# Weighted sum of two expert outputs: first loads of 16, 12, 16 and 4 tokens, merged stores of the late tiles, and a split after 108 tokens

## The chip, the cores and the metric

The kernel runs on one core of one Trainium2 chip. The metric is device time in microseconds of one execution, the median of the runs. The work is done by VectorE (DVE), ScalarE (ACT) and the core's 16 DMA engines; SyncE (SP) and ACT issue the transfers, each on a queue of its own. TensorE is not used.

## The reference

```python
expert_outputs = np.random.randn(16, 1024, 2, 512).astype(np.float32)
combine_weights = np.random.randn(16, 1024, 2).astype(np.float32)

def reference(expert_outputs, combine_weights):
    weights = combine_weights[..., np.newaxis]
    return np.sum(expert_outputs * weights, axis=2).astype(np.float32)
```

For each of 16,384 tokens two rows of 512 numbers are scaled by two weights and added. The kernel reads 67.1 MB of rows and writes 33.6 MB of sums; the weights are 131 KB.

## The kernel before

Each of the 128 partitions takes 128 tokens. A token is 4 KB of input (its two rows side by side) and 2 KB of output. `rows` (the function that cuts a tensor in DRAM) makes two regions: in the first, partition p has the tokens 120p to 120p + 119, so that the rows of two neighbouring partitions start 480 KB apart in the input and 240 KB apart in the output; in the second, the last 1,024 tokens of the tensor are dealt out eight to a partition.

The tokens of a partition go through SBUF in 11 tiles: ten of 12 tokens (`J`) and a last one of 8 (`LAST`). A tile lies in a room `et` of 48 KB in each partition. There are four rooms (`bufs=4`), used in turn, so tile g lies in the room of tile g - 4, and its load has to wait until the store of tile g - 4 has read that room.

The loads are issued on SP, line 75. The first tile has two, one of 2 tokens, cut into 4 KB pieces (`max_dma_last_dim`), and one of 10; every other tile has one, in which each partition's part is a single row of 48 KB (of 32 KB in the last tile).

At the start ACT issues a small store of zeros into places of the output that are written again later (line 58), then the weights in two transfers: those of 120 tokens, 960 B in each partition, and those of the last 8, 64 B (line 62). The first multiply on VectorE waits for the first tile's loads and for the first of these.

A tile g below 9 is combined by two instructions on VectorE. Line 84 multiplies the whole room in place with the weights, each of which is repeated 512 times by the access pattern; line 85 adds the two halves of each token and writes the sums, packed, into the front half of the same room (`ot`). Then ACT issues the store of 12 tokens, a row of 24 KB in each partition (line 86).

In tile 9 ACT scales the first half of each of 12 tokens (line 92), VectorE multiplies the second halves (line 107) and adds (line 108). In tile 10 ACT scales the first half of each of 8 tokens (line 92 again), and VectorE does the rest, one instruction per token (line 96). The stores of these two tiles are issued on SP (line 109), the last two transfers of the program.

The order on each engine is that of the program for the most part; a scheduler may move an instruction (it puts ACT's store of tile 8 among tile 9's scalings).

Of the kernel before, what the change touches and what calls it, by code (L numbers as in the profile page):

```python
# [1 line left out]

# [4 lines left out]


@with_exitstack
def kernel(  # L10
    ctx: ExitStack,
    tc: tile.TileContext,
    expert_outputs: bass.AP,
    combine_weights: bass.AP,
    out: bass.AP,
):

    nc = tc.nc  # L20
    b, s, k, h = expert_outputs.shape
    assert k == 2
    n = b * s
    P = nc.NUM_PARTITIONS
    per = n // P
    assert per * P == n
    J, LAST = 12, 8
    main = per - LAST
    assert main % J == 0
    eo = expert_outputs.rearrange("b s k h -> (b s) (k h)")  # L30
    cw = combine_weights.rearrange("b s k -> (b s) k")
    o = out.rearrange("b s h -> (b s) h")

    def rows(x):

        a = x[0 : P * main, :].rearrange("(p t) f -> p t f", p=P)
        b = x[P * main : n, :].rearrange("(p t) f -> p t f", p=P)
        return lambda t, c: a[:, t : t + c, :] if t < main else b[:, t - main : t - main + c, :]

    eo, cw, o = rows(eo), rows(cw), rows(o)  # L40

    dt = mybir.dt.float32
    mult = mybir.AluOpType.mult
    add = mybir.AluOpType.add
    copy = mybir.ActivationFunctionType.Copy

    last = main // J

    wpool = ctx.enter_context(tc.tile_pool(name="w", bufs=1))
    ipool = ctx.enter_context(tc.tile_pool(name="in", bufs=4))  # L50

    wt = wpool.tile([P, per * k], dt)


    zt = wpool.tile([16, 128], dt)
    nc.vector.memset(zt, 0.0)  # L56
    first = out.rearrange("b s h -> (b s) h")[0 : P * main, :].rearrange("(q t) h -> q (t h)", q=16)
    ahead = nc.scalar.dma_start(out=first[:, 0:128], in_=zt)  # L58

    with tc.issue_after(ahead.ins):  # L60
        for t, c in ((0, main), (main, LAST)):
            nc.scalar.dma_start(
                out=wt[:, k * t : k * (t + c)].rearrange("p (t k) -> p t k", k=k), in_=cw(t, c)
            )
        warm = wpool.tile([P, 1], dt)
        nc.scalar.activation(out=warm, in_=nc.const_aps.tensor(1.0, (P, 1), dt), func=copy)  # L66

    for g in range(last + 1):
        et = ipool.tile([P, J, k * h], dt)

        ot = et.rearrange("p j f -> p (j f)")[:, 0 : J * h].rearrange("p (j f) -> p j f", f=h)
        t0, c = g * J, J if g < last else LAST

        for a, m in ((0, 2), (2, c - 2)) if g == 0 else ((0, c),):
            nc.sync.dma_start(  # L75
                out=et[:, a : a + m],
                in_=eo(t0 + a, m),
                max_dma_last_dim=k * h * 4 if g + a == 0 else None,
            )
        if g < last - 1:  # L80

            wb = wt[:, g * J * k : (g + 1) * J * k].unsqueeze(2).to_broadcast([P, J * k, h])
            ek = et.rearrange("p j (k h) -> p (j k) h", k=k)
            nc.vector.tensor_tensor(out=ek, in0=ek, in1=wb, op=mult)  # L84
            nc.vector.tensor_tensor(out=ot, in0=et[:, :, 0:h], in1=et[:, :, h : 2 * h], op=add)  # L85
            nc.scalar.dma_start(out=o(t0, c), in_=ot)
            continue


        for i in range(c):  # L90
            t = t0 + i
            nc.scalar.activation(  # L92
                out=et[:, i, 0:h], in_=et[:, i, 0:h], func=copy, scale=wt[:, 2 * t : 2 * t + 1]
            )
            if g == last:
                nc.vector.scalar_tensor_tensor(  # L96
                    out=ot[:, i, :],
                    in0=et[:, i, h : 2 * h],
                    scalar=wt[:, 2 * t + 1 : 2 * t + 2],
                    in1=et[:, i, 0:h],  # L100
                    op0=mult,
                    op1=add,
                )
        if g < last:
            w1 = wt.rearrange("p (t k) -> p t k", k=k)[:, t0 : t0 + c, 1:2]
            x1 = et[:, :, h : 2 * h]
            nc.vector.tensor_tensor(out=x1, in0=x1, in1=w1.to_broadcast([P, c, h]), op=mult)  # L107
            nc.vector.tensor_tensor(out=ot, in0=et[:, :, 0:h], in1=x1, op=add)  # L108
        nc.sync.dma_start(out=o(t0, c), in_=ot[:, 0:c])


# [1 line left out]
_INS = ['expert_outputs', 'combine_weights']  # L113
_OUTS = [((16, 1024, 512), 'float32')]


# [23 lines left out]
```

## Time and profile before

| what | value |
|---|---|
| median of 3 runs | 239.1 us (239.07 to 240.33) |
| span of the profiled execution | 237.3 us |
| VectorE busy | 194.1 us, 29 instructions |
| ScalarE busy | 14.0 us, 22 instructions |
| DMA | 100.80 MB, mean 425 GB/s |
| first load issued by SP | 0.72 us |
| first multiply on VectorE | 18.46 us |
| first store of sums issued by ACT | 38.04 us |
| last load landed | 219.82 us |
| last store issued by SP | 226.46 us |

The costliest groups of instructions and some transfers, as the profile has them (line, engine, operation, tiles and shapes, count, then busy time and the mean of one in ns, then the idle time before them and what ended it; for transfers the size of each and the median time from issue to landing):

```profile
L84 DVE TENSOR_TENSOR et<-et,wt 128x12288 f32<-128x12288 f32 x9 | 116.6, 12955 | 24.1 <-DMA wt<-in_combine_weights_dram 17.5
L85 DVE TENSOR_TENSOR et<-et 128x6144 f32<-128x6144 f32 x9 | 59.0, 6557 | 0.3
L92 ACT ACTIVATE et<-et,wt 128x512 f32<-128x512 f32 x20 | 12.5, 708 | 208.6 <-DMA et<-in_expert_outputs_dram 208.6
L96 DVE SCALAR_TENSOR_TENSOR et<-et,wt 128x512 f32<-128x512 f32 x8 | 5.6, 746 | 3.9 <-ACT et L92 3.6
...
et<-in_expert_outputs_dram SPq DMA_DIRECT2D x9, 6144.0 KB, 29.9
out_dram<-et ACTq DMA_DIRECT2D x9, 3072.0 KB, 33.0
```

The span is what the profiler saw of one execution; the time of a run has some more around it, so the median stands above the span. Beside instructions the trace has a record of every DMA packet: one row of one partition on one of the 16 engines, with its start, its duration and its size. Where the prediction speaks of the time of a row, it is from these records.

### The profile page before, as it was taken

The page shows a single profiled execution, that of the slowest core. Times are in us where ns is not written, and L with a number is a line of the kernel's source. Part 1 is how long each engine was busy: PE and PEld are TensorE (multiplying, and loading weights), DVE is VectorE, ACT ScalarE, POOL GpSimd, SP SyncE. Part 2 cuts the span into 40 slices and gives each one's busy share as a digit, 9 for nine tenths or more (in the row PEclk, how much of TensorE's full clock was granted, in tenths as well). Part 3 has the DMA queues.
Part 4 walks back from the last instruction along what each step waited for, and adds up shares of the span by engine and source line. Part 5 has one row for each costly group of instructions (what it writes and reads, how often), then busy time and mean ns, then how long its engine had stood idle before and what let it go on. Part 6 is the DMA issues. An engine that isn't in the chain of part 4 may idle for free.

```text
span 237.3 us, 157 instructions
## 1 busy us (share of the span) xinstructions
DVE 194.1 (82%) x29; ACT 14.0 (6%) x22; POOL 0.2 (0%) x4
## 2 busy tenths in 40 slices
DVE  0008999999999999999999889969996998785710
ACT  2000000000000000000000000000000000740800
POOL 0000000000000000000000000000000000000000
DMA  7999999989899999999898999999998979999997
GB/s 289 452 474 398 398 448 480 398 356 505 352 443 435 427 464 464 398 398 530 348 514 348 447 418 443 464 464 398 398 522 348 522 344 451 464 398 442 406 434 309
DMA packets 3760, 100.80 MB, mean 425 GB/s; under 512 B 544, under 2 KB 688, under 8 KB 944
## 3 DMA queue, kind: packets, MB, share of 16 engines
q1 hardware_dynamic: 2144, 72.35, 71.0%
q10 hardware_dynamic: 1616, 28.45, 27.9%
HBM read 67.24 MB, written 33.56 MB: 425 GB/s over the span
## 4 chain that ended last, share of the span: by engine, by line
DMA 59%; DVE 34%; ACT 2%; ACTq 0%; DVEq 0%; issue 0%; SPq 0%
DMA out_dram<-et 29%; DMA et<-in_expert_outputs_dram 23%; DVE et L84 22%; DVE et L85 11%; DMA wt<-in_combine_weights_dram 7%; ACT et L92 2%; DVE et L96 1%; DVEq L135 0%; ACTq L135 0%; ACTq L58 0%; DVE zt L56 0%; DVEq L84 0%; SPq L75 0%; ACTq L92 0%
## 5 line engine op out<-in xcount | busy, mean ns | idle before, releaser
L84 DVE TENSOR_TENSOR et<-et,wt 128x12288 f32<-128x12288 f32 x9 | 116.6, 12955 | 24.1 <-DMA wt<-in_combine_weights_dram 17.5
L85 DVE TENSOR_TENSOR et<-et 128x6144 f32<-128x6144 f32 x9 | 59.0, 6557 | 0.3
L92 ACT ACTIVATE et<-et,wt 128x512 f32<-128x512 f32 x20 | 12.5, 708 | 208.6 <-DMA et<-in_expert_outputs_dram 208.6
L96 DVE SCALAR_TENSOR_TENSOR et<-et,wt 128x512 f32<-128x512 f32 x8 | 5.6, 746 | 3.9 <-ACT et L92 3.6
L107 DVE TENSOR_TENSOR et<-et,wt 128x6144 f32<-128x6144 f32 x1 | 6.6, 6557 | 2.3 <-DMA et<-in_expert_outputs_dram 2.3
L108 DVE TENSOR_TENSOR et<-et 128x6144 f32<-128x6144 f32 x1 | 6.6, 6558 | 0.9 <-ACT et L92 0.9
L66 ACT ACT_TABLE_LOAD x1 | 1.3, 1283 | 2.4 <-issue 2.4
L56 DVE MEMSET zt<- 16x128 f32 x1 | 0.2, 165 | 0.8 <-PEq L124 0.8
L66 ACT ACTIVATE warm<-const-float32-1.0 128x1 f32<-128x1 f32 x1 | 0.2, 202 | 0.0
L124 POOL MEMSET const-bfloat16-1.0<- 128x1 bf16 x1 | 0.1, 102 | 0.0
L124 POOL MEMSET const-uint8-127<- 128x1 uint8 x1 | 0.1, 101 | 0.0
L124 POOL MEMSET const-float32-0.0<- 128x1 f32 x1 | 0.1, 99 | 0.2 <-issue 0.2
L124 POOL MEMSET const-float32-1.0<- 128x1 f32 x1 | 0.1, 98 | 0.0
## 6 DMA issues: line engine op xcount, KB each, us to landing
et<-in_expert_outputs_dram SPq DMA_DIRECT2D x9, 6144.0 KB, 29.9
out_dram<-et ACTq DMA_DIRECT2D x9, 3072.0 KB, 33.0
et<-in_expert_outputs_dram SPq DMA_DIRECT2D x1, 5120.0 KB, 17.0
et<-in_expert_outputs_dram SPq DMA_DIRECT2D x1, 4096.0 KB, 25.1
out_dram<-et SPq DMA_DIRECT2D x1, 3072.0 KB, 14.6
out_dram<-et SPq DMA_DIRECT2D x1, 2048.0 KB, 10.0
et<-in_expert_outputs_dram SPq DMA_DIRECT2D x1, 1024.0 KB, 5.0
wt<-in_combine_weights_dram ACTq DMA_DIRECT2D x1, 120.0 KB, 17.0
```

What stands on the lines that cost most here:

```text
L56: nc.vector.memset(zt, 0.0)
L66: nc.scalar.activation(out=warm, in_=nc.const_aps.tensor(1.0, (P, 1), dt), func=copy)
L84: nc.vector.tensor_tensor(out=ek, in0=ek, in1=wb, op=mult)
L85: nc.vector.tensor_tensor(out=ot, in0=et[:, :, 0:h], in1=et[:, :, h : 2 * h], op=add)
L92: nc.scalar.activation(out=et[:, i, 0:h], in_=et[:, i, 0:h], func=copy, scale=wt[:, 2 * t : 2 * t + 1])
L96: nc.vector.scalar_tensor_tensor(out=ot[:, i, :], in0=et[:, i, h : 2 * h], scalar=wt[:, 2 * t + 1 : 2 * t + 2], in1=et[:, i, 0:h], op0=mul ...
L107: nc.vector.tensor_tensor(out=x1, in0=x1, in1=w1.to_broadcast([P, c, h]), op=mult)
L108: nc.vector.tensor_tensor(out=ot, in0=et[:, :, 0:h], in1=x1, op=add)
L124: nc = _bacc.Bacc("TRN2", target_bir_lowering=False, num_devices=1)
```

## The change

- The split of the tokens moves: 108 tokens of a partition lie in the first region and 20 in the second (`LAST = 20`). Rows in the first region now start 432 KB apart in the input and 216 KB apart in the output.
- The four rooms are one tile `et` of 48 tokens. They are filled first by loads of 16, 12, 16 and 4 tokens (`FIRST`), which don't end where tiles end. The first load is no longer cut into 4 KB pieces.
- The weights of the first 108 tokens are loaded on SP, right after the first load; those of the last 20 on ACT.
- The sums of tiles 7 and 8 are written side by side into one room and stored by one transfer of 24 tokens; those of tiles 9 and 10 likewise, by one of 20. Both are issued on SP. Tiles 0 to 6 are stored on ACT as before.
- Tile 9 is combined token by token (ACT scales, VectorE multiplies and adds), and tile 10 by ACT's scalings, one multiply and one add; before it was the other way round.
- The order is that of the program on every engine (`manual_schedule`).

```diff
-    J, LAST = 12, 8
+    ROOM, ROOMS = 12, 4
+    TILES = [12, 12, 12, 12, 12, 12, 12, 12, 12, 12, 8]
+    FIRST = [16, 12, 16, 4]
+    STORES = [[0], [1], [2], [3], [4], [5], [6], [7, 8], [9, 10]]
+    WHOLE = [0, 1, 2, 3, 4, 5, 6, 7, 8]
+    MIXED = [10]
+    LAST = 20
...
+    et = pool.tile([P, ROOMS * ROOM, k * h], dt)
+    halves = et.rearrange("p j (k h) -> p (j k) h", k=k)
...
+    def load(t, c, **kw):
+        at = place(t)
+        assert place(t + c - 1) == at + c - 1
+        nc.sync.dma_start(out=et[:, at : at + c], in_=eo(t, c), **kw)
...
+    def combine(g, base):
+        at, c, t0 = g % ROOMS * ROOM, TILES[g], starts[g]
+        if g in WHOLE or g in MIXED:
+            room = halves[:, k * at : k * (at + c), :]
+            x0, x1 = et[:, at : at + c, 0:h], et[:, at : at + c, h : 2 * h]
+            if g in WHOLE:
+                wb = wt[:, k * t0 : k * (t0 + c)].unsqueeze(2).to_broadcast([P, k * c, h])
+                nc.vector.tensor_tensor(out=room, in0=room, in1=wb, op=mult)
+            else:
+                for i in range(c):
+                    x = et[:, at + i, 0:h]
+                    nc.scalar.activation(out=x, in_=x, func=copy, scale=wt[:, k * (t0 + i) : k * (t0 + i) + 1])
+                w1 = wk[:, t0 : t0 + c, 1:2].to_broadcast([P, c, h])
+                nc.vector.tensor_tensor(out=x1, in0=x1, in1=w1, op=mult)
+            nc.vector.tensor_tensor(out=halves[:, base : base + c, :], in0=x0, in1=x1, op=add)
+            return
+        for i in range(c):
+            t = k * (t0 + i)
+            x0, x1 = halves[:, k * (at + i), :], halves[:, k * (at + i) + 1, :]
+            nc.scalar.activation(out=x0, in_=x0, func=copy, scale=wt[:, t : t + 1])
+            nc.vector.scalar_tensor_tensor(
+                out=halves[:, base + i, :], in0=x1, scalar=wt[:, t + 1 : t + 2], in1=x0, op0=mult, op1=add
+            )
...
+        for i, c in enumerate(FIRST):
+            load(t, c, **({} if i == 0 else {}))
+            t += c
+            if i == 0:
+                weights(nc.sync, 0, main)
...
+        for j, st in enumerate(STORES):
+            base, c = st[0] % ROOMS * ROOM * k, 0
+            for g in st:
+                combine(g, base + c)
+                c += TILES[g]
+            assert c <= k * ROOM
+            q = nc.sync if j in (7, 8) else nc.scalar
+            q.dma_start(out=o(starts[st[0]], c), in_=halves[:, base : base + c, :])
+            for g in st:
+                if g + ROOMS < len(TILES):
+                    load(starts[g + ROOMS], TILES[g + ROOMS])
```

More of the change, by code (lines that the diff above doesn't have):

```diff
@@ L26 @@
     assert per * P == n
-    J, LAST = 12, 8
+    ROOM, ROOMS = 12, 4
[5 more added lines that the diff above has]
+    LAST = 20
+    assert sum(TILES) == per and [g for st in STORES for g in st] == list(range(len(TILES)))
     main = per - LAST
[L29 to L32, printed above, removed]
+    starts = [sum(TILES[:g]) for g in range(len(TILES))]
     def rows(x):
[L36 to L40, printed above, removed]
+        first = x[0 : P * main, :].rearrange("(p t) f -> p t f", p=P)
+        second = x[P * main : n, :].rearrange("(p t) f -> p t f", p=P)
+        return lambda t, c: first[:, t : t + c, :] if t < main else second[:, t - main : t - main + c, :]
+    flat = out.rearrange("b s h -> (b s) h")
+    eo = rows(expert_outputs.rearrange("b s k h -> (b s) (k h)"))
+    cw = rows(combine_weights.rearrange("b s k -> (b s) k"))
+    o = rows(flat)
     dt = mybir.dt.float32
@@ L45 @@
     copy = mybir.ActivationFunctionType.Copy
[L47 to L63, printed above, removed]
-            )
-        warm = wpool.tile([P, 1], dt)
-        nc.scalar.activation(out=warm, in_=nc.const_aps.tensor(1.0, (P, 1), dt), func=copy)
@@ L68 @@
[L68 to L109, printed above, removed]
@@ new lines, with place @@
+    pool = ctx.enter_context(tc.tile_pool(name="all", bufs=1))
+    et = pool.tile([P, ROOMS * ROOM, k * h], dt)
+    halves = et.rearrange("p j (k h) -> p (j k) h", k=k)
+    wt = pool.tile([P, per * k], dt)
+    wk = wt.rearrange("p (t k) -> p t k", k=k)
+    zt = pool.tile([16, 128], dt)
+    warm = pool.tile([P, 1], dt)
+    def place(t):
+        g = max(g for g in range(len(TILES)) if starts[g] <= t)
+        return g % ROOMS * ROOM + t - starts[g]
+    def load(t, c, **kw):
+        at = place(t)
+        assert place(t + c - 1) == at + c - 1
+        nc.sync.dma_start(out=et[:, at : at + c], in_=eo(t, c), **kw)
@@ new lines, in weights @@
+    def weights(q, t, c):
+        q.dma_start(out=wk[:, t : t + c, :], in_=cw(t, c))
+    def combine(g, base):
[20 more added lines that the diff above has]
+                out=halves[:, base + i, :], in0=x1, scalar=wt[:, t + 1 : t + 2], in1=x0, op0=mult, op1=add
+            )
@@ new lines @@
+    with tc.manual_schedule():
+        nc.vector.memset(zt, 0.0)
+        ahead = flat[0 : P * main, :].rearrange("(q t) h -> q (t h)", q=16)
+        nc.scalar.dma_start(out=ahead[:, 0:128], in_=zt)
+        weights(nc.scalar, main, per - main)
+        nc.scalar.activation(out=warm, in_=nc.const_aps.tensor(1.0, (P, 1), dt), func=copy)
+        t = 0
+        for i, c in enumerate(FIRST):
[3 more added lines that the diff above has]
+                weights(nc.sync, 0, main)
+        assert t == sum(TILES[:ROOMS])
+        for j, st in enumerate(STORES):
[9 more added lines that the diff above has]
+                    load(starts[g + ROOMS], TILES[g + ROOMS])
```

## The prediction

> **What bounds the kernel now.** I read the page's slices and DMA queues first, then windows, then who waited for whom, and last the chain.
>
> ```profile
> span 237.3 us, 157 instructions
> ...
> DMA  7999999989899999999898999999998979999997
> ...
> q1 hardware_dynamic: 2144, 72.35, 71.0%
> q10 hardware_dynamic: 1616, 28.45, 27.9%
> HBM read 67.24 MB, written 33.56 MB: 425 GB/s over the span
> ```
>
> The two queues' packets fill 71.0 + 27.9 = 98.9% of 16 DMA engines' span, 234.7 of 237.3 us. The kernel is a full pipe: 2.6 us of the span are without packets.
>
> ```profile
> 0.00:6.00 6.00, 0.17 (x1) 1.49 (x2) 0.20 (x4) 1.00 0.78 285
> ...
> 40.00:48.00 8.00, 8.00 (x1) 0.00 (x0) 0.00 (x0) 1.00 0.98 393
> 48.00:60.00 12.00, 11.96 (x3) 0.00 (x0) 0.00 (x0) 1.00 0.99 426
> 60.00:120.00 60.00, 59.87 (x7) 0.00 (x0) 0.00 (x0) 1.00 1.00 433
> 120.00:200.00 80.00, 73.28 (x8) 0.00 (x0) 0.00 (x0) 1.00 1.01 437
> ...
> 220.00:237.30 17.30, 5.57 (x8) 4.91 (x8) 0.00 (x0) 1.00 0.91 391
> ```
>
> The columns are the stretch, its length, DVE, ACT and POOL busy time, clock, DMA share and GB/s. From 60 to 200 us the share is 1.00 or more, and nothing can be gained there but the bytes themselves. What is not full is the first 6 us (first packet at 1.79 us), a dip at 40 to 48 us, and the last 1.2 us (last packet ends at 236.1).
>
> ```profile
> DVE et L84 <- DMA wt<-in_combine_weights_dram: 17.5, 1, 17.5
> DVE et L84 <- DMA et<-in_expert_outputs_dram: 6.6, 3, 2.2
> DVE et L107 <- DMA et<-in_expert_outputs_dram: 2.3, 1, 2.3
> ```
>
> After its start at 18.46 us VectorE waits for loads 6.6 + 2.3 = 8.9 us in all. That is its slack.
>
> ```profile
> 76.96 30.61 DMA out_dram<-et
> ...
> 107.63 29.93 DMA et<-in_expert_outputs_dram
> ...
> 157.24 37.42 DMA out_dram<-et
> ...
> 194.71 25.11 DMA et<-in_expert_outputs_dram
> ```
>
> The chain runs store, load, store, load: a room is stored, then refilled. A 3 MB store takes 30 us only because its packets share the pipe with loads. The length of these pieces is the pipe's, so I cost the change in packets, not in waits.
>
> **Packets.** Every transfer has 128 rows, 8 on each engine. The trace's packet records give the median time of a row: 4 KB 159 ns (mean 194), 16 KB 611, 24 KB 912, 32 KB 1,213, 40 KB 1,514, 48 KB 1,815; a row of weights of 64 B 11 and of 960 B 44. Loads and stores of one size agree. These lie on a line: 9 ns and 36.74 ns per 1,000 B. So a 64 KB row (65,536 B) is estimated at 2,417 ns.
>
> **The change part by part, per DMA engine.**
>
> Removed: sixteen 4 KB rows (the first two tokens) 16 x 194 = 3.11 us; eight 40 KB rows 12.11; sixteen of 72 loads of 48 KB 29.04; twenty-four of 80 store rows of 24 KB 21.89; eight store rows of 16 KB 4.89; weights 8 x (44 + 11) = 0.44. Sum 71.48 us.
>
> Added: sixteen 64 KB rows 38.67; eight load rows of 16 KB 4.89; eight store rows of 48 KB 14.52; eight of 40 KB 12.11; weights of 864 and 160 B, by the line 8 x (41 + 15) = 0.45. Sum 70.64 us. Net -0.84 us.
>
> Of that, 16 x (194 - 159) = 0.56 us are slow first packets: some took about 1,000 ns at 1.8 us, when the pipe starts. Long first rows may pay part of this too. So the ends are -0.28 (all comes back) and -0.84 (none); I take -0.5, as a start is paid once by a long row, but twice or more by short ones.
>
> The price of a 64 KB row is not in the trace. Low end: the line. If it goes as two of 32 KB, 2 x 1,213 = 2,426, which adds 0.15 us over sixteen. High end: the slowest rows of the trace, 30 of 48 KB, mostly around 41 and 47 us, near 2,100 ns, 0.3 above the median; 16 x 0.3 = 4.8 us. I take the line, which six sizes fit, and keep 4.8 for the rival.
>
> **VectorE's start.** The weights of tiles 0 to 8 move from ACT's queue to SP's, behind the 16-token load. Now they land when that load does: 1.79 + 8 x 2.417 + 0.33 for the weights and about 0.9 from packet to semaphore, 22.4 us, and some 0.2 for the slow start: 22.6, against 18.46. On SP the later loads stand behind both, but nothing on SP waits there: three are issued at once, and the fourth, of four tokens, waits for the first to land, with 28 tokens still queued. VectorE is 4.1 us later, paid from its 8.9 us of slack. The first store goes at 22.6 + 19.5 = 42.1 instead of 38.04; the pipe is covered until then by first loads of 25.2 MB, which take up to 59 us. If this cover were gone, 4.1 us. Splitting tiles over loads (tile 1 needs loads one and two, tile 2 loads two and three) delays tile 2's wait a little; VectorE reaches tile 2 at 61.5 us and by then that load, 23.1 MB with half a store between, is in at about 60. Cost: nothing, under the same cover.
>
> VectorE's own work is 9 x (12.955 + 6.557) + 12 x 0.746 + 2 x 4.37 = 193.3 us against 194.1. ACT has 20 scalings as before. Stores of tiles 0 to 6 stay on ACT's queue. The refills of rooms wait for the same seven stores. Merged stores free no room that a load needs, since only loads 4 to 10 follow, after stores 0 to 6.
>
> **The end.** From tile 7 on ACT's queue is empty, so SP's alone must fill the pipe. Load 10 goes out when store 6 has landed (194.66 before). After that point load 9 had three rows of 48 KB left on each engine, 5.4 us, and load 10 is ready 1.07 us after its issue: no gap, with 4 us to spare, which store 7 filled before. Behind load 10 SP issues the store of tiles 7 and 8 (8 x 1.815 = 14.5 us), then that of 9 and 10 (8 x 1.514 = 12.1). SP waits for tile 8's sum with nothing behind it but that last store, which is later anyhow. With the last packet at 236.1 - 0.5 = 235.6, load 10's packets end near 209.0 and it lands at 209.9 (219.82 before). From there ACT's eight scalings take 5.0 us (eight in 5.01 in the timeline), alongside the multiply of 6.557 x 8/12 = 4.37; then the add, 4.37. The last store is issued at 209.9 + 9.5 = 219.4 and ready 1.07 later (0.72 to 1.79 at the start), 220.5. The 24-token store keeps the pipe busy until 209.0 + 14.5 = 223.5. So this stage costs nothing, with 3.0 us to spare. Tile 9's twelve sums on VectorE start at about 200 (tile 8 loaded at about 180.5, then 19.5) and end at 209: in time, but with little over, and they eat from the same 3 us. Without that cover the idle time would be 10.6 us.
>
> **Pitch.** Rows in HBM now lie 432 KB apart instead of 480 KB, and those of the output 216 instead of 240 KB. Packets at 480 KB show no contention from 60 to 200 us, share 1.00. Bounds: 0, and 1.9% of the loads' 156 us of packets, 3.0 us; 1.9% is what separates the span's 425 GB/s from the 433 of 60 to 120 us, the nearest thing to a slower pipe that this trace has. I take 0.
>
> The Trainium skill (DMA: Bandwidth & Descriptors, Latency and other measured facts) speaks of HBM row pitch: at large powers of two, 512 KiB among them, copies lose rate, 207 against 214 GB/s, and an odd few KiB restores it. No run here shows a pitch of 512 KiB. [...]
>
> Sum: 237.3 - 0.5 = 236.8 us of span. The median lies 1.8 above the span (239.1 - 237.3), and this stays: 238.6 us.
>
> **Rivals.**
> 1. The start and the dip both go: -0.84, and the slow rows near 41 to 47 us, which sum to 0.6 us per engine over the median, don't come again: -1.4, 237.7 us. For it: they stand once, where the first store begins, and that moment moves by 4 us. Against: a first store there will still be.
> 2. Reads are slower in the new shape (64 KB rows, 432 KB pitch). Place: every load, the first 60 us most. Price 3.0 us on all loads, or 4.8 on the long rows: 241.6 to 243.4 us. From 1.7 us on (1.1% of the loads, or 0.11 us for each long row) it decides. For it: neither shape has been seen in this trace, and the dip shows that rows can be slow. Against: six sizes on one line.
> 3. The last store comes late. Place: 219 to 224 us. If tile 9's and 10's sums are 3 us later than worked out the pipe empties, and each further microsecond is one on the end; at 6 us late 238.6 + 3 = 241.6. Against: VectorE still has 4.8 us of slack ahead.
> 4. The change does nothing in the pipe: merged stores move the same bytes. It is the forecast's own upper end, 238.8.
>
> **How the numbers follow.** About 0.5% (1.2 us) is what a measurement of this kernel tells from no change: 237.9 to 240.3 counts as the same. Forecast, with rival 4 in it, 0.46, its own range 238.0 to 239.4; rival 1, 0.24; rival 2, 0.20; rival 3, 0.10. The time is the forecast's, 238.6. The range goes from 237.3 (rival 1 less 0.4 between chips) to 241.8 (rivals 2 and 3 at their lower prices), which leaves some 0.15 out. Faster 0.24, same 0.46, slower 0.30.
>
> **What would show it.** Right: shares of the two queues summing to 98.9% or more; the first multiply at 22 to 23 us; waits of VectorE for loads down from 8.9 to about 4 to 5 us; the last load landed near 210, the last store issued near 219, and full slices to the end. Wrong: a slice under 9 tenths near 223 us (rival 3), GB/s under 420 in 2 to 60 us with full shares (rival 2), or a first 6 us with a share near 0.9 and no dip at 40 to 48 (rival 1).

## The result, and the profile after

The changed kernel takes 239.85 us (median of 18 runs, 239.59 to 240.93) against 239.13 before (18 runs): 1.0031 times as long, 95% interval 1.0023 to 1.0039. That is 0.72 us slower, where 0.5 us faster was forecast, and inside the 0.5% that was called no change. The span of the profiled execution grew from 237.3 to 237.8 us; the other 0.2 to 0.3 us lie outside it. Of all 129 runs of the kernel before, ten took 240.1 to 240.8 us and the others 239.0 to 239.5, so medians are compared.

The page after: span, busy share of the DMA engines in 40 slices, the two queues, and the bytes.

```profile
span 237.8 us, 156 instructions
...
DMA  9897999999899999999999999999898999999995
...
q1 hardware_dynamic: 2016, 78.75, 77.2%
q10 hardware_dynamic: 1184, 22.05, 21.6%
HBM read 67.24 MB, written 33.56 MB: 424 GB/s over the span
```

The shares still sum to 98.8%, though 560 packets fewer are moved (512 rows and 48 packets of 4 B): 0.988 x 237.8 = 234.95 us of packets against 234.77. Fewer rows did not make the pipe shorter. The last slice fell from 7 to 5 tenths, but that is not the loss: a packet counts in the slice in which it starts, the last rows are now 40 KB instead of 16 KB long, and the first experiment below has the same 5 at a span of 237.3 us.

The windows after (stretch, length, DVE, ACT and POOL busy, clock, DMA share, GB/s):

```profile
0.00:6.00 6.00, 0.17 (x1) 1.49 (x2) 0.20 (x4) 1.00 0.92 350
...
40.00:48.00 8.00, 8.00 (x2) 0.00 (x0) 0.00 (x0) 1.00 1.08 417
48.00:60.00 12.00, 11.96 (x2) 0.00 (x0) 0.00 (x0) 1.00 0.88 378
60.00:120.00 60.00, 59.77 (x7) 0.00 (x0) 0.00 (x0) 1.00 1.00 432
120.00:200.00 80.00, 76.73 (x9) 0.00 (x0) 0.00 (x0) 1.00 1.00 433
200.00:220.00 20.00, 19.04 (x15) 12.47 (x20) 0.00 (x0) 1.00 1.00 431
```

Here too a packet counts where it starts, and one 64 KB row on each of 16 engines is 1 MB, so the rate of a short stretch hangs on where it is cut: from 40 to 60 us these lines give 394 GB/s against 413 before, but from 36 to 56 us the same view gives 422 against 393. With each packet spread over its own duration both cuts agree: 413 GB/s from 40 to 60 us against 421 before, which is 0.4 us of the pipe. From 60 to 220 us it is 433 in both. The place to look is the first mixing of stores with loads.

Waits after, and the end of the timeline (start, length, engine, line, operation):

```profile
DVE et L83 <- DMA wt<-in_combine_weights_dram: 22.3, 1, 22.3
DVE et L83 <- DMA et<-in_expert_outputs_dram: 3.1, 2, 2.2
```

```profile
202.09 18.16 SPq L122 DMA_DIRECT2D out_dram<-et  x2
210.41 5.01 ACT L87 ACTIVATE et<-et,wt 128x512 f32<-128x512 f32 x8 [2.25 <-DMA et<-in_expert_outputs_dram]
210.42 4.43 DVE L89 TENSOR_TENSOR et<-et,wt 128x4096 f32<-128x4096 f32 x1
215.45 4.43 DVE L90 TENSOR_TENSOR et<-et 128x4096 f32<-128x4096 f32 x1 [0.60 <-ACT et L87]
```

The second wait fell from 6.6 + 2.3 to 3.1 us: VectorE paid its late start from its slack. The last load has landed at 210.3, and the last store, the second of the two on line 122, is issued at 219.90, while the 24-token store is still on the engines (until 224.4 us). There is no gap at the end.

The packet records give the ledger, in us per DMA engine. "By the line" is every row at 9 ns plus 36.74 ns per 1,000 B; "first rows" and "stall" are what rows before 8 us and after it took above that (rows over by more than 25 ns, nearly all beside the first store of sums).

```
                 by the line   first rows   stall    span
before             233.59         0.56       0.57    237.3
after              233.27         0.66       0.99    237.8
```

The saving by the line, 0.32 us, is there. The first rows cost 0.10 more, and the stall 0.42 more. The first packet starts 0.05 earlier, and the program ends 0.10 later after the last packet. The rest, 0.2 us, is not split further here: the last packets of the engines end 0.54 us apart instead of 0.43, and packets overlap by less. From 10 to 230 us 16 or more packets are under way all the time, before and after.

What else changed is that the engines no longer keep step. The semaphore records show that one transfer is reported done by the first and the last of the 16 engines 0.46 us apart before (every transfer from 75 to 196 us within 0.02 of that), and after, 1.5 to 2.2 us apart; this distance is called the spread below. The packet records show the same: before, the stores go in rounds, and between one round and the next no store row is under way for 1.37 us or more, from 44 to 200 us. In the changed kernel these pauses are 1.06 to 1.57 us until 60 us; from then on most are 0.36 us, as the rounds are stretched.

### The profile page after: what moved, and what is told of

The parts are those of the page before. It is cut to its first block, busy times and chain, and to the rows that moved or that the text cites. A ratio compares the mean times of both kernels' runs of the same rounds, so it can differ in the third digit from the quotient of the medians.

```text
span 237.8 us, 156 instructions
## 1 busy us (share of the span) xinstructions
DVE 192.3 (81%) x33; ACT 14.0 (6%) x22; POOL 0.2 (0%) x4
## 4 chain that ended last, share of the span: by engine, by line
DVE 53%; DMA 30%; issue 6%; ACT 2%; ACTq 0%; SPq 0%; another core or an unknown queue 0%; DVEq 0%
DVE et L83 38%; DVE et L90 15%; DMA out_dram<-et 15%; DMA wt<-in_combine_weights_dram 9%; DMA et<-in_expert_outputs_dram 6%; ACT et L87 2%; ACTq L151 0%; SPq L71 0%; DVEq L83 0%; ACTq L87 0%
## 5 line engine op out<-in xcount | busy, mean ns | idle before, releaser
L90 DVE TENSOR_TENSOR et<-et 128x6144 f32<-128x6144 f32 (+1 forms) x10 | 63.4, 6345 | 0.9 <-ACT et L87 0.6
L96 DVE SCALAR_TENSOR_TENSOR et<-et,wt 128x512 f32<-128x512 f32 x12 | 8.2, 745 | 0.2
L89 DVE TENSOR_TENSOR et<-et,wt 128x4096 f32<-128x4096 f32 x1 | 4.4, 4426 | 0.0
```

Of the source, the lines that this page charges most:

```text
L89: nc.vector.tensor_tensor(out=x1, in0=x1, in1=w1, op=mult)
L90: nc.vector.tensor_tensor(out=halves[:, base : base + c, :], in0=x0, in1=x1, op=add)
L96: nc.vector.scalar_tensor_tensor(out=halves[:, base + i, :], in0=x1, scalar=wt[:, t + 1 : t + 2], in1=x0, op0=mult, op1=add)
```

## The experiments

All edits are to the changed kernel unless said otherwise. Where several parts of the change were undone in a diff, only the changed lines are shown. The kernel before ran beside each, at 239.12 to 239.15 us.

**Four kernels that each undo or change one part**

```diff
-    FIRST = [16, 12, 16, 4]
+    FIRST = [12, 12, 12, 12]
```

> Only the first fill is undone: four loads of 12 tokens (48 KB rows) instead of 16, 12, 16 and 4; the weights still follow the first load on SP. In the profile of the changed kernel the packets around the first store of sums (42 to 51 us) take 0.99 us per engine more than their usual time, against 0.56 us before; the loads there are 64 KB rows. Theory A (the stall at the first store grows with the length of the load rows beside it): stall back to about 0.55 us, time 239.85 - 0.43 = 239.4 us. Theory B (the pitch of 432 and 216 KB makes it longer): stall stays near 1.0 us, time 239.8. Theory C (the merged stores at the end cost it): time 239.8. By theory A and B alike the first multiply starts near 18.3 us instead of 23.3.

Measured 239.42 us (1.0019 of before, 1.0002 to 1.0037), stall 0.49. The number is theory A's, and so the fill holds 0.43 us of the loss by the medians. Seven of the 12 runs lie below every run of the changed kernel; the other five took 240.2 to 240.7, so this run alone would not settle it, but the same fill has a low stall again twice below. That it is the length of the rows is not shown by this.

```diff
-    STORES = [[0], [1], [2], [3], [4], [5], [6], [7, 8], [9, 10]]
-    LAST = 20
+    STORES = [[0], [1], [2], [3], [4], [5], [6], [7, 8], [9], [10]]
+    LAST = 8
...
-            q = nc.sync if j in (7, 8) else nc.scalar
+            q = nc.sync if j in (7, 8, 9) else nc.scalar
```

> The split goes back to 120 and 8 tokens, so rows lie 480 and 240 KB apart again; first loads of 16, 12, 16 and 4 stay, tiles 7 and 8 stay merged, and tiles 9 and 10 are stored one by one, since they now lie in two regions. Theory B (pitch): the stall at the first store falls from 0.99 to about 0.56 us per engine, time about 239.4 us. Theory A (long load rows): the stall stays near 1.0 us, time 239.8. Theory C (merged stores): about half of 0.3 us goes, 239.7.

Measured 239.84 us (1.0025, 1.0013 to 1.0036), stall 0.69 (0.42 of it before 60 us), spread of landings 1.65 us. Beside the first store the stall fell as far as theory B says, but the time did not move, and below the old pitch stands beside this fill with a stall of 1.02: the old pitch brings nothing back, and theory B falls.

```diff
-    STORES = [[0], [1], [2], [3], [4], [5], [6], [7, 8], [9, 10]]
+    STORES = [[0], [1], [2], [3], [4], [5], [6], [7], [8], [9], [10]]
...
-            q = nc.sync if j in (7, 8) else nc.scalar
+            q = nc.sync if j in (9, 10) else nc.scalar
```

> Every tile is stored by itself: tiles 0 to 8 from ACT, 9 and 10 from SP, as before; the first fill and the split after 108 tokens stay. Theory C (the long last rows of 40 KB cost at the end of the span and after it: engines end 0.27 us apart instead of 0.21, and the time is 2.05 us above the span instead of 1.8): 239.85 - 0.3 = 239.5 us. Theories A and B: 239.85, since the stall near 42 to 51 us is untouched.

Measured 240.12 us (1.0041, 1.0023 to 1.0059). Single stores are slower by 0.27 us, not faster, though the intervals overlap. But this kernel does not test theory C alone, since it has a gap at its end:

```profile
213.63 17.58 SPq L122 DMA_DIRECT2D out_dram<-et  x2
...
226.41 4.42 DVE L90 TENSOR_TENSOR et<-et 128x4096 f32<-128x4096 f32 x1 [0.60 <-ACT et L87]
```

With the stores of tiles 7 and 8 single and on ACT's queue, the load of tile 10 lands at 221.3 us instead of 210.3. The last store is issued at 230.87, and between 230 and 234 us the engines are without a packet for 0.42 us each. The stall is 0.78, 0.35 of it before 60 us, and the spread 1.66. What fells theory C is that merged stores reach a span of 237.3 with other fills (the first experiment, and the fill of before, below).

```diff
-    zt = pool.tile([16, 128], dt)
+    zt = pool.tile([P, 128], dt)
...
-        ahead = flat[0 : P * main, :].rearrange("(q t) h -> q (t h)", q=16)
+        ahead = flat[0 : P * main, :].rearrange("(q t) h -> q (t h)", q=P)
```

> The small store of zeros at the start touches the first 512 B of all 128 partitions' output rows instead of 16 places; all of it is written again later. Theory D (the stall comes from the first write into each partition's stretch of the output): with every stretch touched before, the 0.99 us per engine near 42 to 51 us goes, 239.85 - 0.9 = 238.9 us. Theory E (it comes from the first mixing of loads and stores, or from the first large store on ACT's queue): the stall stays, 239.9 us.

Measured 240.13 us (1.0033, 1.0018 to 1.0048), stall 1.00. Touching every stretch of the output beforehand leaves the stall as it was, and the time is 0.28 us above the changed kernel's, with intervals that overlap: theory D falls.

**The fill again, the end's code, and the small store**

```diff
-    FIRST = [16, 12, 16, 4]
+    FIRST = [12, 12, 4, 4, 4, 4, 4, 4]
```

> The first fill is 12, 12 and then six loads of 4 tokens, so the loads beside the first store of sums (from about 38 us) have 16 KB rows. With 48 KB rows there (first fill 12, 12, 12, 12) the stall was 0.49 us per engine and the time 239.42 us; with 64 KB rows 0.99 and 239.85. Theory A (the stall grows with the length of the load rows beside the first store): stall about 0.15 to 0.25 us; 32 more rows per engine at 9 ns give 0.29 back, so the time is about 239.4. Theory A2 (the stall is a fixed cost of the first store, and 48 against 64 KB was chance): stall 0.5 us or more, time 239.7.

Measured 241.43 us (1.0093, 1.0077 to 1.0108), stall 1.61, spread 2.4 us. (Only four runs.) Theory A falls here: the shortest rows beside the first store had one of the longest stalls (39 rows of 16 KB there took 0.44 us too long on average). It is also the slowest but one of all.

```diff
-    FIRST = [16, 12, 16, 4]
+    FIRST = [16, 16, 4, 12]
```

> First fill 16, 16, 4, 12: the long rows stay and so does the late first multiply (near 23.3 us), but beside the first store (from about 43 us) lie rows of 16 and 48 KB. Theory A: stall 0.2 to 0.5 us, time 239.85 - 0.6 = about 239.3 us. Theory A3 (long rows, or the late start of VectorE, cost wherever they stand): stall near 1.0, time 239.85.

Measured 240.07 us (1.0044, 1.0031 to 1.0056), stall 1.07, spread 1.9. Theory A misses again, and A3's stall came.

```diff
-    FIRST = [16, 12, 16, 4]
-    MIXED = [10]
+    FIRST = [12, 12, 12, 12]
+    MIXED = [9]
```

> First fill 12, 12, 12, 12, and tiles 9 and 10 are combined as before the change: tile 9 by twelve scalings, a multiply and an add, tile 10 token by token, so VectorE has 4 fewer instructions. All versions built on the changed kernel run 2.05 us above their span, the kernel before 1.8. Theory F (that 0.25 us belongs to the longer code of the end): 239.42 - 0.25 = 239.17 us at the same span of 237.3. Theory G (it belongs to something that all of them share, the order by hand or the one big tile): 239.4.

Measured 239.24 us (1.0009, 0.9995 to 1.0023): no different from before. Its runs lie 1.78 us above their span, those of the first experiment 2.06. The time fell by 0.18, near the 0.25 of theory F.

```diff
-    FIRST = [16, 12, 16, 4]
+    FIRST = [12, 12, 12, 12]
...
-        nc.scalar.dma_start(out=ahead[:, 0:128], in_=zt)
```

> First fill 12, 12, 12, 12, and the small store of zeros at the start is left out. Theory D2 (the stall beside the first store of sums is a cost of the first write to HBM, which the small store takes in part): stall grows from 0.49 to 1 us or more, time 239.9 or more. Theory E (it is the first mixing of loads with stores): stall 0.5, time 239.4.

Measured 239.46 us (1.0017, 1.0006 to 1.0027), stall 0.45, against 239.42 and 0.49 with it. The small store does nothing here, and theory D2 falls.

**Both sides**

This one is an edit to the kernel before:

```diff
     zt = wpool.tile([16, 128], dt)
+    pad = wpool.tile([16, 8], dt)
+    for i in range(6):
+        nc.vector.memset(pad[:, i : i + 1], 0.0)
     nc.vector.memset(zt, 0.0)
```

> The kernel before with six memsets of one number each on VectorE at the start, where it waits for 17.5 us anyhow: its records on VectorE go from 48 to 54, the number of the changed kernel. Runs with 54 records there lie 2.05 us above their span, those with 44 and 48 lie 1.78. Theory F (what lies outside the span follows the number of VectorE's instructions): span as before, 237.3, outside 2.05, time 239.4 us. Theory G (it comes from something else of the changed kernel): 239.13 us.

Measured 239.41 us, its 12 runs from 239.34 to 239.54. (The interval of the ratio, 0.9991 to 1.0017, is pulled by two long runs of the kernel before, 240.2 and 240.8; the other 27 end at 239.27, below every run of this kernel.) Its page:

```profile
span 237.4 us, 163 instructions
...
DVE 194.3 (82%) x35; ACT 14.0 (6%) x22; POOL 0.2 (0%) x4
```

The span is that of before, with 0.2 us more VectorE work in a wait; the time is 2.04 us above it, before 1.79. Six idle memsets cost 0.29 us, all of it where the profile doesn't look. Theory F holds as a step and not as a slope: up to 48 records on VectorE (44 and 48 alike) 1.78, at 54 2.05. Why it is so no run shows.

```diff
-    MIXED = [10]
+    MIXED = [9]
```

> The changed kernel with only the ways in which tiles 9 and 10 are combined exchanged again (44 records on VectorE instead of 54). Theory F: outside the span 1.78 instead of 2.06, span near 237.8, time 239.6 us. If the tail mattered instead, with tile 10 done token by token the last store would be issued later or earlier than 219.9 us; about 220.5 is expected, and no gap.

Measured 239.90 us (1.0024, 1.0009 to 1.0039): outside the span 1.77, as theory F has it, but the span of the runs has a median of 238.1 instead of 237.8 (stall 1.12), which takes the gain back. The last store is issued at 221.06 us, with the 24-token store still on the engines: no gap. Whether the other end or chance lengthened the span is not shown. With this fill it differs from one execution to the next: the changed kernel's 18 spans go from 237.5 to 238.9, while 27 of 32 of before's are 237.3 or 237.4.

```diff
-    FIRST = [16, 12, 16, 4]
+    FIRST = [16, 16, 16]
```

> First fill of three equal loads of 16 tokens: 64 KB rows throughout, a late first multiply (near 23.3 us) and tiles that need two loads, as in the change, but no row sizes that differ within the fill. Theory U (loads of unequal length in the fill put the DMA engines out of step and lengthen the stalls): stall 0.5 us per engine, time 239.4. Theory L (a first store that comes late, beside long rows, is what costs): stall 0.9 us or more, time 239.8.

Measured 241.69 us (1.0107, 1.0074 to 1.0140), stall 1.61, spread up to 5.6 us. Theory U falls: equal rows throughout, and the slowest kernel of all. Its page:

```profile
span 239.7 us, 157 instructions
...
DMA  9898989989999999998999999999999999999993
```

The last slice is 3 tenths full, where the changed kernel has 5: the engines report the last store done 2.27 us apart, and the slowest sets the time. Only 0.42 us of the stall lies before 60 us, the rest from 60 to 150.

```diff
-    STORES = [[0], [1], [2], [3], [4], [5], [6], [7, 8], [9, 10]]
-    MIXED = [10]
-    LAST = 20
+    STORES = [[0], [1], [2], [3], [4], [5], [6], [7], [8], [9], [10]]
+    MIXED = [9]
+    LAST = 8
...
-            q = nc.sync if j in (7, 8) else nc.scalar
+            q = nc.sync if j in (9, 10) else nc.scalar
```

> Of the change only the first fill (16, 12, 16, 4, weights behind the first) and the order by hand are left: split after 120 tokens, every tile stored by itself, tiles 9 and 10 combined as before. Theory U or L (the fill is what costs): span up by 0.4 to 0.5 us, outside 1.78, time 239.5 to 239.6. If it takes fill and pitch together: 239.1.

Measured 239.63 us (1.0017, 1.0002 to 1.0032), outside the span 1.79, stall 1.02, spread 2.1 (both from an execution of 240.30 us, the longest of its 12). The fill alone costs 0.5 us in a kernel that but for the order by hand, the one tile and the weights' queue is the one before, and with four loads of 12 these three cost nothing that can be told (239.24 us): both sides agree.

**Which property of the fill**

Four kernels with `MIXED = [9]`. The first and the last also have this, which reads the weights and writes a tile that nothing reads:

```diff
+    late = pool.tile([P, 1024], dt)
...
+        for i in range(5):
+            w0 = wt[:, 0:1].to_broadcast([P, 1024])
+            nc.vector.tensor_tensor(out=late, in0=w0, in1=w0, op=mult)
         for j, st in enumerate(STORES):
```

With `FIRST = [12, 12, 12, 12]` and the extra multiplies:

> First fill 12, 12, 12, 12 and tiles 9 and 10 combined as before (239.24 us, stall 0.48 us per engine, landings of one transfer spread over 0.7 us among the engines), with five multiplies of 1,024 numbers on VectorE, which nothing reads, between the weights' landing and the first tile: the first store goes about 5 us later, near 43. Theory L (a late first store costs): stall near 1.0, time 239.7. Theory V (loads of unequal length, or shared by tiles, cost): stall 0.5, time 239.24, plus 0.27 if five more instructions on VectorE show outside the span.

Measured 240.71 us (1.0062, 1.0042 to 1.0082), stall 0.85, spread 2 to 3.4 us. The extra work took 6.3 us, and the first store went at 44.25. Its page, and that of the same kernel without the delay:

```profile
span 238.8 us, 152 instructions
...
DMA  7999999999999989999999999899999999999994
```

```profile
span 237.4 us, 148 instructions
...
DMA  7999999999899999999999999999999998999995
```

No slice is empty, yet the span is 1.4 us longer. From the packet records, after 234 us the engines stand without a packet for 0.84 us more each (2.54 against 1.70), since they end 1.9 us apart instead of 0.7. Of the stall only 0.23 us lies before 60 us and 0.62 between 72 and 90, so it did not grow at the first store. With this fill a late first store costs by itself, and more than theory L said.

With `FIRST = [12, 12, 16, 8]` and no extra multiplies:

> First fill 12, 12, 16, 8 and tiles 9 and 10 combined as before: the first store is on time, near 38 us, the rows beside it are of 64 KB, and tiles 2 and 3 share a load. Theory V: landings spread over 1.4 us or more from 62 us on, as in the changed kernel, stall 0.8 to 1.0, time 239.7. Theory L: as with four loads of 12, 239.24 us, spread 0.7.

Measured 239.72 us (1.0023, 1.0010 to 1.0036), stall 1.20, spread 2.2. Theory V's number: with the first store on time, unequal rows cost too.

With the fill and the queues of before:

```diff
-        weights(nc.scalar, main, per - main)
+        weights(nc.scalar, 0, main)
+        weights(nc.scalar, main, per - main)
...
-    FIRST = [16, 12, 16, 4]
+    FIRST = [2, 10, 12, 12, 12]
...
-            load(t, c, **({} if i == 0 else {}))
+            load(t, c, **({"max_dma_last_dim": k * h * 4} if i == 0 else {}))
...
-            if i == 0:
-                weights(nc.sync, 0, main)
```

> The fill of before (2 tokens in 4 KB rows, 10, 12, 12, 12; weights on ACT) and tiles 9 and 10 combined as before: what is left of the change is the split after 108 tokens, the merged stores and the order by hand. By the prediction's ledger these save 24 + 8 short store rows for 16 long ones, 0.15 us of row overhead at most: 239.0 us. If the long last rows or the pitch cost by themselves, 239.4 or more.

Measured 239.05 us against 239.15 beside it, ratio 1.0011 (0.9991 to 1.0031), stall 0.63, spread 0.46. By the medians the split after 108 tokens and the merged stores cost nothing, and their saving of at most 0.1 us is under what can be told apart. It has the lowest median of all, and is not shown to beat the kernel before: four of its 12 runs took 240.3 to 240.7 us, of before's only two of 29.

With `FIRST = [12, 12, 16, 8]` and the extra multiplies:

> First fill 12, 12, 16, 8 with the five extra multiplies: late store and unequal rows together, as in the change. Theory L and theory V alike: stall near 1.0, time 239.7 (+ 0.27 if the instructions show). If only both together cost, this one alone of the three new fills is slow.

Measured 239.23 us (1.0017, 0.9989 to 1.0045), with runs from 239.05 to 243.75: seven of the 12 at 239.05 to 239.23, five at 239.7 or more. The profiled one took 240.15, with a spread of 0.94 and a stall of 0.74. Both properties together mostly cost nothing, and at times much. So neither "late" nor "unequal" is the cause as such.

What the slow fills share is the spread. Of every profiled execution, the median spread of landings from 75 to 196 us, the stall, and the span; last, the median span of all runs of that kernel:

```
fill                                       spread   stall   span    all runs
before, six memsets                         0.45    0.61    237.4    237.4
before                                      0.46    0.57    237.3    237.3
2, 10, 12, 12, 12 (merged stores)           0.46    0.63    237.3    237.3
12, 12, 12, 12 (no small store)             0.50    0.45    237.3    237.4
12, 12, 12, 12                              0.55    0.49    237.3    237.4
12, 12, 12, 12 (tail of before)             0.68    0.48    237.4    237.5
12, 12, 16, 8 (late start)                  0.94    0.74    238.4    237.5
16, 12, 16, 4 (pitch of before)             1.65    0.69    237.9    237.8
16, 12, 16, 4 (single stores)               1.66    0.78    237.9    238.1
16, 12, 16, 4 (tail of before)              1.85    1.12    238.1    238.1
16, 16, 4, 12                               1.88    1.07    238.0    238.0
16, 12, 16, 4 (128 outputs touched)         2.01    1.00    238.1    238.1
16, 12, 16, 4 (the change)                  2.02    0.99    237.8    237.8
16, 12, 16, 4 (alone)                       2.14    1.02    238.5    237.9
12, 12, 16, 8                               2.15    1.20    238.1    238.0
12, 12, six of 4                            2.43    1.61    239.3    239.2
16, 16, 16                                  2.49    1.61    239.7    239.6
12, 12, 12, 12 (late start)                 2.76    0.85    238.8    239.0
```

Up to 0.7 us of spread the span is 237.3 to 237.4, from 1.6 to 2.2 us it is half a microsecond or more longer, and above 2.4 about one and a half or more. The row at 0.94 doesn't fit: its spread is small in the middle, but its engines end 1.6 us apart. The six profiles with the fill of the change and the six with that of before or four loads of 12 on time don't overlap in spread, stall or span. The spread is a mark of the slow fills; that it causes the time is not shown, and by the packets under way no engine is without one for more than 0.01 us in all from 10 to 230 us, in any of these profiles.

In the change the spread begins with the first store: 0.68 us for the load that lands at 38 us, 1.39 for the one at 62.

## Why the prediction was wrong

**The step that failed first** is "Cost: nothing, under the same cover", said of VectorE's late start and of the new fill. The cover was right: the pipe was never without packets until 59 us. But a full pipe is not a pipe at its rate. Where the first store of sums meets the loads, rows took longer than the line (0.99 us per engine instead of 0.57), and from 84 to 195 us the engines ran 1.5 to 2.2 us apart. Undoing the fill in the changed kernel took off 0.43 us; putting it alone into the kernel before put on 0.5. The trace of before had shown the stall, 0.6 us, as a dip at 40 to 48 us; I priced only its going (rival 1) or its return for long rows (rival 2, 0.3 us a row), never that the new fill could make it larger. Which side of the fill does it, the late start or the row lengths, the runs leave open.

**The second** is "The median lies 1.8 above the span, and this stays". It became 2.05. The changed tail gives VectorE four more of the short instructions and six more records, and six memsets in the kernel before did the same (239.41 us). 0.27 us of the 0.72 was there.

**Mis-sized**: the net of the rows. Of -0.84 I let -0.5 stand, as a long first row should pay the slow start only once. The 4 KB rows paid 0.56 us in all, the 64 KB rows 0.66. All of it came back, so the term was -0.32 by the line plus 0.10, about -0.2.

Some smaller things don't come out either. Rival 4, no change in the pipe, would be 239.1 us and not 238.8. The upper end 241.8 is above both prices that it names, 241.6. No run shows the 0.4 us between chips: on four chips the kernel before had medians of 239.12 to 239.15. That the measured time lies inside the range and counts as no change is luck as far as the mechanism goes, since the stall and the time outside the span, 0.7 us together, were both put at nothing.

**Right**: the price of a 64 KB row away from the two bad places (median 2,418 ns, 2,417 by the line). The end: last load at 210.3 (209.9 foretold), last store issued at 219.90 (219.4), no gap, so rival 3 didn't happen, though tile 9's sums ended at 210.4 instead of 209, just as VectorE could start on tile 10. VectorE's start was 23.29 instead of 22.6, 0.7 later than worked out (the slow first rows took 0.66 us, where 0.2 was allowed), and its waits fell to 3.1 us, less than the 4 to 5 foretold. The pitch: 480 KB brought back in the change gave 239.84, the same; and 432 KB beside the old fill 239.05. The Trainium skill's rule on HBM row pitch (DMA: Bandwidth & Descriptors, Latency and other measured facts) names large powers of two, and these two pitches, which are none, show no difference; no run here tried one that is.

**Rival 1** had the right place and the wrong sign. **Rival 2** was right that rows could be slow, but they cost 0.42 us per engine and not 3.0 or more, and neither pitch nor length explains it: 16 KB rows fared no better than those of 64 KB. Its sign, under 420 GB/s from 2 to 60 us, came up all the same (416, counted where packets start; before 429). Spread over the packets' durations it is 420 against 423.

**Open**: what puts the engines out of step. A late store did it with rows of 48 KB, and rows of 16 and of 64 KB did it with an early one; late and unequal together mostly did not. By the skill's account (the same page, Queues, rings and completion order) each engine takes turns between the queues, a packet at a time, on its own. The packet records agree: from 100 to 140 us of the changed kernel 234 rows of 24 KB to store and 239 of 48 KB to load start, about one for one. Engines that enter the alternation at different points would land a transfer a row apart, which fits spreads of about 2 us (one load row is 1.8 us), but why that slows the rows themselves is not shown. The pauses between rounds of store rows, which shrink to 0.36 us after 60 us in the changed kernel and stay in the kernel before, fit this too. Touching the output before, or leaving out the first small store, had no part in it.

## What to carry to other kernels

In a kernel whose DMA engines are full, look for the places where rows take longer than their size says, and at how far apart the engines report one transfer done; a change of the first loads can cost there without any empty slice. Compare the time with the span as well as the spans with each other, since instructions that cost nothing inside the span, as they run in a wait, can cost outside it. Two changes that each cost something need not cost more together, so test parts from both sides.

## What the runs showed of the hardware that was not expected

- Six memsets of one number on VectorE, run in a wait of 17.5 us, lengthened the time by 0.29 us and the span by less than 0.1. With 44 or 48 records on VectorE the time lay 1.78 us above the span, with 54 2.05; with 56, and five more on SP, 2.2.
- In all 18 profiles rows beside the first store of sums take longer than their usual time, by 0.2 to 1.2 us per engine in all between 8 and 60 us. Later stores start after pauses of ACT's queue too (3.2 us with no store row under way, seven times in the kernel before, and 3.5 us at 82 us in the changed one), and rows there keep their usual time; in other kernels rows after 60 us are slow too (0.27 us in all with the old pitch, 1.20 with 16, 16, 16).
- A delay of 6.3 us on VectorE, which in the kernel before had 8.9 us of waits to spend, cost 1.5 us (240.71 against 239.24). VectorE did not set the end: the last store was issued at 221.69 us, with the 24-token store still on the engines. The stall grew by 0.37 us, and the DMA engines finished 1.9 us apart instead of 0.7.
